# Sliding-window matmul on one core: other row blocks for the weight loads, and the last two k tiles split into two column halves

## Chip, core and metric

The kernel runs on one core of one Trainium2 chip. The metric is device time in microseconds of that core. The kernel before took 182.32 us in the median of three runs (182.32 to 182.44).

## The reference

```python
B, S, D, W = 4, 4096, 4096, 64          # x: [B, S, D] fp32, w: [D, D] fp32
for b in range(B):
    o = int(offsets[b])
    results.append(x[b, o:o+W] @ w)     # 64 rows of each batch times one 4096 x 4096 matrix
return np.stack(results)
```

There are only 256 rows of x, so every element of w is used 256 times and then dropped. The kernel must read 67.1 MB of w and 4.2 MB of x, and write 4.2 MB.

## The kernel before

Two groups g of 128 rows (two batches each) are transposed on PE. The weights stream from HBM, cast to fp16 by the load. k tiles 0 to 21 come in whole rows, in blocks of up to four k tiles; their products are added to an fp32 accumulator in SBUF on DVE. For the last ten k tiles ("tail") the columns are split into two groups of 2048, and each of the eight PSUM banks collects a whole tail.

```python
blocks = [(0, 1), (1, 1), (2, 4), (6, 4), (10, 4), (14, 4), (18, 2), (20, 2)]
k_tail = 22
wc_pool = ctx.enter_context(tc.tile_pool(name="wc", bufs=3))     # 4 k tiles each
w1_pool = ctx.enter_context(tc.tile_pool(name="w1", bufs=2))     # 1 k tile each
# ...
order = [1, 0]                       # column group 1 first, group 0 last
for ng in order:
    # ... loads on the GpSimd queue, two k tiles each; the last two of group 0 one by one
for ng in order:
    # ... matmuls: for ki, for g, for j (four banks for each g)
    for g in range(G):
        for j in range(n_sub):
            add_out(4 * g + j, g, ng * n_sub + j)            # acc += bank, on DVE
    for g in range(G):
        (nc.gpsimd if ng == order[0] else q[g]).dma_start(   # q = [nc.scalar, nc.sync]
            out=out[2 * g : 2 * g + 2, :, ng * NG : (ng + 1) * NG],
            in_=acc[g][:, ng * NG : (ng + 1) * NG],
        )
```

The stores of group 1 are issued on GpSimd, in the queue that holds the remaining loads. The stores of group 0 are the very last work, on ACT and SP.

## Time and profile before

| | before |
|---|---|
| time | 182.32 us |
| span in the profile | 180.4 us |
| PE / DVE / ACT busy | 127.1 / 79.2 / 14.4 us |
| share of the GpSimd DMA queue | 94.2% of 16 engines |
| HBM read / written | 71.30 / 4.19 MB |

Busy time of an engine says how much it did, not whether it was waited for. PE is busy for 70% of the span but waits for loads again and again. Time to landing runs from issue to the last engine's completion, so it includes queueing. And a stretch gives a mean of 16 engines, while a landing shows the latest of them.

### The profile page before, as it was taken

What the parts mean: (1) busy time and instruction counts of PE and PEld (TensorE: products, weight loads), DVE (VectorE), ACT (ScalarE), POOL (GpSimd) and SP (SyncE); (2) the same over time, 40 slices, a digit from 0 to 9 for tenths busy, and PEclk for the clock granted to TensorE, in tenths of its full rate; (3) what the DMA queues carried; (4) which work ended last, traced back from release to release, by engine and by line L of the source; (5) the groups of instructions that cost most, each with busy time, mean ns of one, the idle gap of its engine ahead of it and who ended that gap; (6) DMA issues with size and microseconds to landing.
All of it is one profiled execution on the core that took longest, in us unless ns stands there. A gap on an engine that the chain in (4) does not pass through costs nothing.

```text
span 180.4 us, 1501 instructions
## 1 busy us (share of the span) xinstructions
PE 127.1 (70%) x576; PEld 57.8 (32%) x576; DVE 79.2 (44%) x120; ACT 14.4 (8%) x19; POOL 15.2 (8%) x30
## 2 busy tenths in 40 slices
PE   0000789504999399908996599999789998898900
PEld 0000774101344144303442244444234443343400
DVE  0000667400587277811886167899920007300280
ACT  2422546400000000000000000000000000000000
POOL 4600000000000100020002400041011001100000
PEclk9999999965799999996999879999999999999975
DMA  5999989999998899999999999999999999999986
GB/s 185 314 254 216 273 189 196 236 233 225 233 233 174 182 233 233 238 218 233 196 196 203 225 207 207 225 193 214 215 213 216 213 214 214 216 212 214 362 367 265
DMA packets 4936, 40.98 MB, mean 227 GB/s; under 512 B 450, under 2 KB 450, under 8 KB 3010
## 3 DMA queue, kind: packets, MB, share of 16 engines
q0 software_dynamic: 4352, 36.70, 94.2%
q1 hardware_dynamic: 288, 2.10, 3.1%
q10 hardware_dynamic: 290, 2.10, 2.8%
q8 instruction: 4, 0.07, 0.1%
q14 instruction: 2, 0.02, 0.0%
HBM read 71.30 MB, written 4.19 MB: 419 GB/s over the span
## 4 chain that ended last, share of the span: by engine, by line
DMA 57%; PE 29%; another core or an unknown queue 5%; issue 3%; DVE 1%; POOLq 1%; POOL 1%; DVEq 1%
DMA wc<-in_w_dram 57%; PE bank L143 29%; DVE acc L153 1%; POOLq L68 1%; DVEq L227 1%; POOL xrow L75 0%; POOL identity masks.py:197 0%; POOLq L75 0%; DVEq L153 0%; POOL w L64 0%; POOLq masks.py:199 0%; POOLq L216 0%
## 5 line engine op out<-in xcount | busy, mean ns | idle before, releaser
L143 PE MATMUL bank<-wc,xT 128*128 128x512 f16 x448 | 106.0, 394 | 25.1 <-DMA wc<-in_w_dram 22.4
L153 DVE TENSOR_TENSOR acc<-acc,bank 128x512 f32<-128x512 f32 x104 | 68.1, 685 | 72.8 <-PE bank L143 72.2
L143 PEld LDWEIGHTS <-xT 128*128 128x128 f16 x512 | 51.2, 101 | 93.6 <-DMA wc<-in_w_dram 23.6
L129 PE MATMUL bank<-identity,xrow 128*128 128x128 f16 x64 | 7.1, 312 | 19.6 <-DMA xrow<-in_x_dram 19.6
L138 DVE CAST xT<-bank 128x512 f16<-128x512 f32 x8 | 5.5, 692 | 21.5 <-PE bank L129 21.5
L143 PE MATMUL bank<-w,xT 128*128 128x512 f16 x64 | 14.6, 385 | 0.0
L129 PEld LDWEIGHTS <-xrow 128*128 128x128 f16 x64 | 6.7, 148 | 19.8 <-issue 19.8
L108 POOL DMA_DIRECT2D wc<-in_w_dram x8 | 5.6, 710 | 42.4 <-PE bank L143 36.0
L92 POOL DMA_DIRECT2D wc<-in_w_dram x6 | 3.2, 545 | 67.7 <-PE bank L143 67.7
L168 DVE COPY acc<-bank 128x512 f32<-128x512 f32 x8 | 5.5, 692 | 1.6 <-PE bank L143 1.4
L140 ACT CAST xT<-bank 128x512 f16<-128x512 f32 x8 | 4.7, 585 | 8.2 <-PE bank L129 8.2
L170 ACT COPY acc<-bank 128x512 f32<-128x512 f32 x8 | 4.7, 585 | 2.5 <-PE bank L143 2.5
L198 POOL DMA_DIRECT2D out_dram<-acc x2 | 1.1, 536 | 18.5 <-DVE acc L153 18.5
L108 POOL DMA_DIRECT2D w<-in_w_dram x3 | 1.8, 607 | 8.6 <-DMA wc<-in_w_dram 8.6
L61 ACT CAST w<-acc 128x2048 f16<-128x2048 f32 x1 | 1.9, 1897 | 4.7 <-DMA acc<-in_w_dram 4.7
L75 POOL DMA_DIRECT2D xrow<-in_x_dram x4 | 2.1, 524 | 2.1 <-issue 2.1
L60 ACT CAST w<-acc 128x2048 f16<-128x2048 f32 x1 | 1.9, 1897 | 2.9 <-DMA acc<-in_w_dram 2.9
L60 ACT ACT_TABLE_LOAD x1 | 1.3, 1283 | 1.8 <-PEq L216 1.8
L64 POOL DMA_DIRECT2D w<-in_w_dram x1 | 0.7, 667 | 0.8 <-POOLq L216 0.8
masks.py:199 POOL TENSOR_SCALAR_AFFINE_SELECT identity<-identity 128x128 f16<-128x128 f16 x1 | 0.3, 287 | 0.1
masks.py:197 POOL MEMSET identity<- 128x128 f16 x1 | 0.2, 223 | 0.0
L216 POOL MEMSET const-float32-0.0<- 128x1 f32 x1 | 0.1, 99 | 0.4 <-issue 0.4
(3 smaller groups left out, 0.3 us busy)
## 6 DMA issues: line engine op xcount, KB each, us to landing
wc<-in_w_dram POOLq DMA_DIRECT2D x4, 4096.0 KB, 48.3
wc<-in_w_dram POOLq DMA_DIRECT2D x8, 1024.0 KB, 36.5
wc<-in_w_dram POOLq DMA_DIRECT2D x2, 2048.0 KB, 38.8
w<-in_w_dram POOLq DMA_DIRECT2D x2, 1024.0 KB, 28.2
xrow<-in_x_dram POOLq DMA_DIRECT2D x4, 512.0 KB, 14.5
out_dram<-acc POOLq DMA_DIRECT2D x2, 1024.0 KB, 19.3
acc<-in_w_dram SPq DMA_DIRECT2D x1, 1024.0 KB, 5.1
acc<-in_w_dram ACTq DMA_DIRECT2D x1, 1024.0 KB, 11.2
```

Of the source, the lines that this page charges most:

```text
L60: nc.scalar.copy(out=w_one[0][:, :NG], in_=w0_32[:, :NG])
L61: nc.scalar.copy(out=w_one[0][:, NG:], in_=w0_32[:, NG:])
L75: nc.gpsimd.dma_start(out=x16[g][m * WIN : (m + 1) * WIN, :], in_=x[b][bass.ds(o, WIN), :],)
L92: nc.gpsimd.dma_start(out=t[:, base : base + r * N], in_=w[k0 * P : (k0 + r) * P, :].rearrange("(p r) n -> p (r n)", r=r),)
L108: nc.gpsimd.dma_start(out=t[:, c : c + n * NG].rearrange("p (t n) -> p t n", t=n), in_=w[ki * P : (ki + n) * P, ng * NG : (ng + 1) * NG].r ...
L129: nc.tensor.matmul(out=ps[t][:, i * P : (i + 1) * P], lhsT=x_cols(g, 4 * t + i), rhs=identity[:], start=True, stop=True,)
L138: nc.vector.tensor_copy(out=dst, in_=ps[t][:])
L140: nc.scalar.copy(out=dst, in_=ps[t][:])
L143: nc.tensor.matmul(out=ps[bank][:], lhsT=xT[g][:, kt * P : (kt + 1) * P], rhs=rhs, start=start, stop=stop,)
L153: nc.vector.tensor_add(out=dst, in0=dst, in1=ps[bank][:])
L168: nc.vector.tensor_copy(out=acc[g][:, c * NT : (c + 1) * NT], in_=ps[bank][:])
L170: nc.scalar.copy(out=acc[g][:, c * NT : (c + 1) * NT], in_=ps[bank][:])
```

## The change

The intent has two parts: fewer, larger loads in whole rows with a shorter tail on fewer buffers, and a shorter end. At the end the last two k tiles are loaded, multiplied, added and stored in two column halves, so that the first half is stored while the second is still being worked on.

```diff
-    blocks = [(0, 1), (1, 1), (2, 4), (6, 4), (10, 4), (14, 4), (18, 2), (20, 2)]
-    k_tail = 22
+    blocks = [(0, 1), (1, 1), (2, 4), (6, 4), (10, 4), (14, 4), (18, 3), (21, 3)]
+    k_tail = 24
+    n_fine = 2
 ...
+    fine_steps.append((n_k - n_fine, n_fine, 0, NG // 2))
+    fine_steps += [(ki, 1, NG // 2, NG) for ki in range(n_k - n_fine, n_k)]
 ...                                      # group 1 is drained by DVE and ACT together:
+            add_out(4 * g + j, g, ng * n_sub + j)
+            nc.scalar.copy(out=tmp[2 * g + j // 2][:], in_=ps[4 * g + j + 1][:])
 ...                                      # group 0, k tiles 30 and 31:
+    for h in range(2):
+        js = range(h * n_sub // 2, (h + 1) * n_sub // 2)
+        for ki in range(k_fine, n_k):
             for g in range(G):
+                for j in js:
+                    tail_mm(ki, g, ng, j, False, ki == n_k - 1)
+        for g in range(G):
+            for j in js:
                 add_out(4 * g + j, g, ng * n_sub + j)
+            c0 = ng * NG + h * NG // 2
+            store(q[g], g, c0, c0 + NG // 2)
```

More of the change, by code (lines that the diff above doesn't have):

```diff
@@ L41 @@
     wc_pool = ctx.enter_context(tc.tile_pool(name="wc", bufs=3))
-    w1_pool = ctx.enter_context(tc.tile_pool(name="w1", bufs=2))
+    w1_pool = ctx.enter_context(tc.tile_pool(name="w1", bufs=1))
     acc_pool = ctx.enter_context(tc.tile_pool(name="acc", bufs=1))
@@ L49 @@
     xT = [x_pool.tile([P, D], fp16, name=f"xT{g}") for g in range(G)]
-    w_one = [w1_pool.tile([P, N], fp16, name="w1", tag="w1") for i in range(2)]
+    w_one = [w1_pool.tile([P, N], fp16, name=f"w1_{i}") for i in range(2)]
+    tmp = [acc_pool.tile([P, NT], fp32, name=f"tmp{i}") for i in range(4)]
     acc = [acc_pool.tile([P, N], fp32, name=f"acc{g}") for g in range(G)]
@@ L84 @@
     }
-    free = 0
     for k0, r in blocks[2:]:
-        if free < r:
-            t = wc_pool.tile([P, R_MAX * N], fp16, name="wc", tag="wc")
-            free = R_MAX
-        base = (R_MAX - free) * N
-        free -= r
+        t = wc_pool.tile([P, R_MAX * N], fp16, name="wc", tag="wc")
         nc.gpsimd.dma_start(
-            out=t[:, base : base + r * N],
+            out=t[:, : r * N],
             in_=w[k0 * P : (k0 + r) * P, :].rearrange("(p r) n -> p (r n)", r=r),
@@ L96 @@
         for q in range(r):
-            src[k0 + q] = lambda a, e, t=t, c=base + q * N: t[:, c + a : c + e]
+            src[k0 + q] = lambda a, e, t=t, c=q * N: t[:, c + a : c + e]
     tail = {}
     order = [1, 0]
-    for ng in order:
-        big = wc_pool.tile([P, R_MAX * N], fp16, name="wc", tag="wc")
-        small = w1_pool.tile([P, N], fp16, name="w1", tag="w1")
-        ki = k_tail
-        while ki < n_k:
-            n = 1 if ng == order[-1] and ki >= n_k - 2 else 2
-            n_in = (ki - k_tail) * NG
-            t, c = (big, n_in) if n_in < R_MAX * N else (small, n_in - R_MAX * N)
+    steps = [(ki, 2, 0, NG) for ki in range(k_tail, n_k, 2)]
+    fine_steps = steps[: -(n_fine // 2)]
+    fine_steps.append((n_k - n_fine, n_fine, 0, NG // 2))
+    fine_steps += [(ki, 1, NG // 2, NG) for ki in range(n_k - n_fine, n_k)]
+    for ng, st in zip(order, (steps, fine_steps)):
+        t = wc_pool.tile([P, R_MAX * N], fp16, name="wc", tag="wc")
+        pos = 0
+        for ki, n, c0, c1 in st:
+            wd = c1 - c0
             nc.gpsimd.dma_start(
-                out=t[:, c : c + n * NG].rearrange("p (t n) -> p t n", t=n),
-                in_=w[ki * P : (ki + n) * P, ng * NG : (ng + 1) * NG].rearrange(
+                out=t[:, pos : pos + n * wd].rearrange("p (t n) -> p t n", t=n),
+                in_=w[ki * P : (ki + n) * P, ng * NG + c0 : ng * NG + c1].rearrange(
                     "(t p) n -> p t n", p=P
@@ L114 @@
             for q in range(n):
-                tail[(ng, ki + q)] = t[:, c + q * NG : c + (q + 1) * NG]
-            ki += n
+                for j in range(wd // NT):
+                    a = pos + q * wd + j * NT
+                    tail[(ki + q, (ng * NG + c0) // NT + j)] = t[:, a : a + NT]
+            pos += n * wd
     def x_cols(g, kt):
@@ L177, with tail_mm @@
     whole_rows(last_block, range(order[1] * n_sub, (order[1] + 1) * n_sub), False)
-    q = [nc.scalar, nc.sync]
-    for ng in order:
-        kts = list(range(k_tail, n_k))
-        if ng == order[0]:
-            kts = list(last_block) + kts
-        for ki in kts:
-            for g in range(G):
-                for j in range(n_sub):
-                    c = ng * n_sub + j
-                    rhs = (
-                        src[ki](c * NT, (c + 1) * NT)
-                        if ki < k_tail
-                        else tail[(ng, ki)][:, j * NT : (j + 1) * NT]
-                    )
-                    mm(4 * g + j, g, ki, rhs, ki == kts[0], ki == kts[-1])
+    def tail_mm(ki, g, ng, j, start, stop):
+        c = ng * n_sub + j
+        rhs = src[ki](c * NT, (c + 1) * NT) if ki < k_tail else tail[(ki, c)]
+        mm(4 * g + j, g, ki, rhs, start, stop)
@@ L194, with store @@
+    out_rows = out.rearrange("b m n -> (b m) n")
+    def store(eng, g, c0, c1, cuts=(0, P)):
+        for a, e in zip(cuts, cuts[1:]):
+            eng.dma_start(out=out_rows[g * P + a : g * P + e, c0:c1], in_=acc[g][a:e, c0:c1])
+    ng = order[0]
+    kts = list(last_block) + list(range(k_tail, n_k))
+    for ki in kts:
         for g in range(G):
             for j in range(n_sub):
-                add_out(4 * g + j, g, ng * n_sub + j)
-        for g in range(G):
-            (nc.gpsimd if ng == order[0] else q[g]).dma_start(
-                out=out[2 * g : 2 * g + 2, :, ng * NG : (ng + 1) * NG],
-                in_=acc[g][:, ng * NG : (ng + 1) * NG],
-            )
+                tail_mm(ki, g, ng, j, ki == kts[0], ki == kts[-1])
@@ new lines @@
+    for g in range(G):
+        for j in range(0, n_sub, 2):
+            add_out(4 * g + j, g, ng * n_sub + j)
+            nc.scalar.copy(out=tmp[2 * g + j // 2][:], in_=ps[4 * g + j + 1][:])
+    for g in range(G):
+        for j in range(1, n_sub, 2):
+            c = ng * n_sub + j
+            dst = acc[g][:, c * NT : (c + 1) * NT]
+            nc.vector.tensor_add(out=dst, in0=dst, in1=tmp[2 * g + j // 2][:])
+        store(nc.gpsimd, g, ng * NG, (ng + 1) * NG)
+    ng = order[1]
+    k_fine = n_k - n_fine
@@ new lines @@
+    for ki in range(k_tail, k_fine):
+        for g in range(G):
+            for j in range(n_sub):
+                tail_mm(ki, g, ng, j, ki == k_tail, False)
+    q = [nc.scalar, nc.sync]
+    for h in range(2):
+        js = range(h * n_sub // 2, (h + 1) * n_sub // 2)
+        for ki in range(k_fine, n_k):
+            for g in range(G):
+                for j in js:
+                    tail_mm(ki, g, ng, j, False, ki == n_k - 1)
+        for g in range(G):
+            for j in js:
+                add_out(4 * g + j, g, ng * n_sub + j)
+            c0 = ng * NG + h * NG // 2
+            store(q[g], g, c0, c0 + NG // 2)
```

## The prediction

> **What bounds the kernel now.** I read the page's slices and DMA queues first, to see which resource has no slack; then the stretches of the last 16 us, then the landing times of the last transfers, and the chain of waits last of all, because a chain shows only one of several paths that end together.
>
> ```profile
> PE   0000789504999399908996599999789998898900
> DVE  0000667400587277811886167899920007300280
> DMA  5999989999998899999999999999999999999986
> HBM read 71.30 MB, written 4.19 MB: 419 GB/s over the span
> ```
>
> The DMA row never falls below 8 between the first slice and the last, while PE and DVE both have empty slices. So the 16 DMA engines carry the kernel from end to end. Loads that cast from fp32 to fp16 count in the GB/s row by what they write, half of what they read. Of the stretches (columns: window, its length, busy us and instructions of PE, PEld, DVE, ACT, POOL, then PE clock, DMA share, GB/s):
>
> ```profile
> 132.00:152.00 20.00, 19.81 (x92) 8.90 (x92) 2.05 (x5) 0.00 (x0) 0.54 (x1) 1.00 1.06 215
> 169.00:172.00 3.00, 2.79 (x13) 1.08 (x11) 1.69 (x3) 0.00 (x0) 0.00 (x0) 1.00 1.01 426
> 172.00:172.50 0.50, 0.00 (x0) 0.00 (x0) 0.50 (x2) 0.00 (x0) 0.00 (x0) 1.00 0.93 393
> 172.50:173.00 0.50, 0.00 (x0) 0.00 (x0) 0.50 (x2) 0.00 (x0) 0.00 (x0) 1.00 0.82 344
> 173.00:173.50 0.50, 0.00 (x0) 0.00 (x0) 0.50 (x2) 0.00 (x0) 0.00 (x0) 1.00 0.31 131
> 173.50:174.00 0.50, 0.00 (x0) 0.00 (x0) 0.50 (x2) 0.00 (x0) 0.00 (x0) 0.98 0.74 311
> 174.00:178.50 4.50, 0.00 (x0) 0.00 (x0) 1.19 (x2) 0.00 (x0) 0.00 (x0) 0.50 1.04 431
> ```
>
> In the middle the engines read 2 x 215 = 430 GB/s, and in the tail of pure stores they move 426 to 431 GB/s: one and the same rate. At it, 71.30 MB of loads and 4.19 MB of stores need 75.49 MB / 430 GB/s = 175.6 us of the span of 180.4 us. Only one hole shows, from 172.0 to 174.0 us: 393 + 344 + 131 + 311 = 1179 where four half microseconds at 431 would give 1724, so 545 / 431 x 0.5 = 0.63 us of the engines' mean time is lost there.
>
> The last transfers, by issue (timeline) and by time to landing (the DMA view of the stretch around each issue; the number at the end is us to landing):
>
> ```profile
> 135.63 0.54 POOL L108 DMA_DIRECT2D w<-in_w_dram  x1 [4.33 <-DMA wc<-in_w_dram]
> w<-in_w_dram POOLq DMA_DIRECT2D x1, 512.0 KB, 34.0
> 152.83 0.54 POOL L198 DMA_DIRECT2D out_dram<-acc  x1 [16.66 <-DVE acc L153]
> 155.22 0.53 POOL L198 DMA_DIRECT2D out_dram<-acc  x1 [1.85 <-DVE acc L153]
> out_dram<-acc POOLq DMA_DIRECT2D x1, 1024.0 KB, 19.3
> 172.83 0.35 ACTq L198 DMA_DIRECT2D out_dram<-acc  x1
> 175.21 0.35 SPq L198 DMA_DIRECT2D out_dram<-acc  x1
> out_dram<-acc ACTq DMA_DIRECT2D x1, 1024.0 KB, 4.2
> out_dram<-acc SPq DMA_DIRECT2D x1, 1024.0 KB, 4.2
> ```
>
> The last load (k tile 31) lands at 135.63 + 34.0 = 169.6 us. The two stores of the first column group, queued behind all loads, land at 172.1 and 174.5; the ACT store lands at 177.0 and the SP store at 179.4. These are steps of 2.4 to 2.5 us, and 1.049 MB at 430 GB/s is 2.44 us. So whichever engine finishes each transfer last had work all the way: the hole of 0.63 us was felt by engines that were ahead, not plainly by the one that sets the landings. From 179.4 to the end of the span is 1.0 us, and 1.9 us more lie between span and the measured 182.32 us.
>
> **What the Trainium skill says.** "DMA: Bandwidth & Descriptors", section "Where 436 GB/s comes from", puts the ceiling of the fabric at 435 GB/s; the trace's 426 to 431 agrees and says that no shuffling of transfers makes the middle faster. Its section "Issuing engines are not separate DMA queues" says that transfers from SP, ACT and GpSimd share the same 16 engines; the trace agrees, the two ACT and SP stores alone fill 174.0 to 178.5 us at 431 GB/s. Its section "Queues, rings and completion order" says that an engine goes round between the queues it has work for, packet by packet: stores issued earlier on ACT and SP will mix with those waiting in the GpSimd queue and push them later rather than end sooner in sum. In "Anatomy of one DMA" (SWDGE path) it gives about 2.0 us fixed plus bytes at 436 GB/s; that makes 4.4 us for 1.049 MB, and the trace has 4.2 us for the ACT and SP stores.
>
> **The change part by part.** (1) *Row blocks 4, 3, 3 in place of 4, 2, 2, tail of 8 k tiles in place of 10.* The bytes stay. Whole-row loads write 216 GB/s in the stretch from 81 to 98 us, the tail's form 215 from 132 to 152 us; moving 2 of 32 k tiles (4.19 MB, 9.75 us) between forms that differ by 0.5% is worth 0.05 us. (2) *Buffers.* The three big buffers now serve blocks 14-17, 18-20, 21-23, then the tail of group 1 waits for PE to finish 14-17 (117.3 us in the timeline) and that of group 0 for 18-20. Block 18-20 lands at 101.3 (the first matmul of block 14-17) + 20 x 3/4 = about 116; its 48 matmuls at 0.226 us (3.62 us for 16 in the timeline) start near 117.3 and end near 128.5. By then the queue holds work to 130.5 (21-23) and to 150 (four loads of 2.10 MB for group 1, 4.87 us each). So the group 0 loads are issued some 20 us before their turn: no starvation. (3) *Draining group 1 through ACT.* Four ACT copies (585 ns each in the page's groups) go beside four DVE adds, then four SBUF adds follow; PE loses less time at the group change, where it waited 12 times 0.22 us. But the next operands land at about 155 us and PE waits for them anyway. The GpSimd stores go out near 157 and 158.5 us instead of 152.8 and 155.2; their turn in the queue comes near 168 us. Worth 0. (4) *The tail in halves.* The three loads of k tiles 30 and 31 end when the two did, near 169.6 us. k tiles 28 and 29 land at 164.6 us; from there PE has the same 32 matmuls x 0.226 us = 7.2 us, ending near 171.9. The first add now follows the 21st of these instead of the 25th, near 169.5 instead of 170.31 us. Eight adds took 4.87 us, so 0.61 each: four end near 171.9, the other four near 174.4. The four half-size stores are issued near 170.8, 172.0, 173.2 and 174.4, in place of two at 172.83 and 175.21. The first enters while the GpSimd stores still drain, so the hole of 0.63 us is filled. Before, the ACT store's bytes began 0.7 us after issue (172.83 against the stretch from 173.5); so the last half has its bytes ready near 175.2. The half microseconds from 167.5 on show 270, 328 and 401 GB/s; with 213 for loads alone and 431 for stores alone, 0.74, 0.47 and 0.14 of them were loads, so the engines turn to stores at 167.5 + 0.5 x 1.35 = 168.2 us on average; by 175.2 they have moved 7.0 us x 430 = 3.0 MB, and 3.67 MB were on offer without the last half. The DMA engines are therefore never short, with 1.5 us to spare, and **the end is set by bytes**: between 0 (the slowest engine had no hole) and 0.63 us (all engines gain equally) earlier. (5) *Costs.* One more load, two more stores, and runs of 4 KB in place of 8 KB for the last two k tiles and the last stores, 4.2 MB together. From 64 KB runs (blocks of 4) to 8 KB runs (tail) the rate fell by the 0.5% of part 1; I put down 1% for this halving, 0.1 us of 9.75. Sum: 0.3 to 0.4 us gained of the hole (my middle between 0 and 0.63), 0.1 lost, nothing elsewhere: about 0.3 us.
>
> **Rivals.** *The tail is a latency chain.* The chain of waits speaks for it:
>
> ```profile
> 164.72 6.22 PE bank L143 x28
> 172.79 2.39 DVE acc L153 x4
> ```
>
> It runs from the last but one load through PE and DVE to the SP store, as if DMA were idle. Then the last issue comes 0.8 us sooner and a store of half the size takes 1.2 us less (2.0 + 1.2 = 3.2 us by the skill's fit, an estimate), and the end is 174.4 + 3.2 = 177.6 in place of 179.4: 1.8 us gained, 180.5 us. The landings at the full rate speak against it. *The queue runs dry in the middle*, because blocks of 3 come free later or a GpSimd issue waits for one of its older transfers. That would cost one step of up to 5 us, some 185 us; the 20 us of depth speak against it. *Smaller packets cost more than I put down.* Loads of 4 KB runs and stores of 4 KB rows carry 4.2 MB; at 5% less rate that is 0.5 us, giving 182.6.
>
> **Range and chances.** The middle is 182.32 - 0.3 = 182.0 us. The hole wholly filled and a little of the latency chain gives 181.3; smaller packets and no gain give 182.7. Faster by 2% would need 3.6 us, twice what the latency rival gives and more than all idle DMA time after 169 us: 2%. Slower by 2% needs a dry queue: 2%. Within 2%: 96%.
>
> **What would show it.** If I am right, the stretches from 172 to 174 us hold 400 GB/s or more, the SP and ACT stores are issued near 171, 172, 173 and 174.5 us, yet take far longer than 3.2 us from issue to landing, because they queue; the last load lands at 169.6 us within 0.3, and the last store between 178.7 and 179.5. I am wrong if the last store lands before 178.3, if a load's landing slips by more than 0.5 us, or if any middle slice of the DMA row falls under 8.

## The result

The changed kernel takes 182.38 us in the median of six runs (182.20 to 182.56), the kernel before 182.32 us (182.16 to 182.44). The ratio is 1.0004, with a 95% interval of 0.9991 to 1.0016. All ratios here are from runs of the same rounds, so they are not quite the ratios of the medians quoted. Medians of different rounds also come from different chips: the kernel before took 182.24 to 182.36 us on those used below. The kernel is correct, and the time is the same.

First the slices and the HBM line of the changed kernel.

```profile
PE   0000779504999399808995699999399999987900
DVE  0000657500578278802876168899374000820460
...
DMA  5999989999999899999989989999999999999994
...
HBM read 71.30 MB, written 4.19 MB: 418 GB/s over the span
```

The DMA row is full as before and the bytes are the same. Now the stretches at the end (columns: window, length, PE, PEld, DVE, ACT and POOL busy, PE clock, DMA share, GB/s), those of the changed kernel first:

```profile
172.00:172.50 0.50, 0.00 (x0) 0.00 (x0) 0.50 (x2) 0.00 (x0) 0.00 (x0) 1.00 0.85 360
172.50:173.00 0.50, 0.00 (x0) 0.00 (x0) 0.50 (x2) 0.00 (x0) 0.00 (x0) 1.00 1.02 426
173.00:173.50 0.50, 0.00 (x0) 0.00 (x0) 0.50 (x2) 0.00 (x0) 0.00 (x0) 1.00 1.01 418
173.50:174.00 0.50, 0.00 (x0) 0.00 (x0) 0.50 (x2) 0.00 (x0) 0.00 (x0) 1.00 0.99 410
...
177.50:178.00 0.50, 0.00 (x0) 0.00 (x0) 0.00 (x0) 0.00 (x0) 0.00 (x0) 0.50 0.85 344
178.00:178.50 0.50, 0.00 (x0) 0.00 (x0) 0.00 (x0) 0.00 (x0) 0.00 (x0) 0.50 0.40 164
178.50:179.00 0.50, 0.00 (x0) 0.00 (x0) 0.00 (x0) 0.00 (x0) 0.00 (x0) 0.50 0.16 66
179.00:179.50 0.50, 0.00 (x0) 0.00 (x0) 0.00 (x0) 0.00 (x0) 0.00 (x0) 0.50 0.04 16
```

And the kernel before in the same last stretches:

```profile
177.50:178.00 0.50, 0.00 (x0) 0.00 (x0) 0.00 (x0) 0.00 (x0) 0.00 (x0) 0.50 1.03 426
178.00:178.50 0.50, 0.00 (x0) 0.00 (x0) 0.00 (x0) 0.00 (x0) 0.00 (x0) 0.50 1.14 475
178.50:179.00 0.50, 0.00 (x0) 0.00 (x0) 0.00 (x0) 0.00 (x0) 0.00 (x0) 0.50 0.21 82
```

The hole of before, with its deepest half microsecond at 131 GB/s, is gone. But a ramp has appeared at the end: 344, 164, 66 and 16 GB/s over the last 2 us, where the kernel before ran at full rate up to 178.5 us. The idle time was moved, not removed.

The trace shows for which engine. It keeps 16 completion counts for each full transfer, one from each engine: a store of 120 rows that is tried below has 15 after its issue, and one of 8 rows has 8. No view prints these counts; they were read from the packed trace, one execution of each kernel. Their first and last, in us:

| | last load | GpSimd stores (group 1) | ACT and SP stores (group 0) |
|---|---|---|---|
| before | 168.05 to 169.63 | 170.55 to 172.12, 173.01 to 174.56 | 176.54 to 177.01, 179.05 to 179.46 |
| changed | 168.21 to 169.81 | 170.72 to 172.27, 173.17 to 174.71 | 174.43 to 175.96, 175.66 to 177.21, 176.93 to 178.47, 178.16 to 179.70 |

The engines run some 1.5 us apart. In the kernel before, the latest count goes from 174.56 to 177.01 us, 2.45 us, like the steps for 1.05 MB around it (2.44 to 2.49): the latest engine had no hole. The earliest count takes 3.53 us for that step: the hole was in the engines that were ahead. In the changed kernel the engines that are ahead no longer wait there, and the 1.5 us stay to the end. The mean of the 16 counts of the last store comes 0.5 us sooner (178.62 in place of 179.16 us), the latest does not (179.70 and 179.46).

Next the issues of the last transfers in the changed kernel (timeline) and, in the second fence, their times to landing (DMA view of the stretch around each).

```profile
140.37 0.54 POOL L108 DMA_DIRECT2D wc<-in_w_dram  x1 [4.50 <-DMA wc<-in_w_dram]
158.35 0.54 POOL L189 DMA_DIRECT2D out_dram<-acc  x1 [17.45 <-DVE acc L205]
159.56 0.53 POOL L189 DMA_DIRECT2D out_dram<-acc  x1 [0.67 <-DVE acc L205]
170.89 2.74 ACTq L189 DMA_DIRECT2D out_dram<-acc  x2
172.08 2.72 SPq L189 DMA_DIRECT2D out_dram<-acc  x2
```

```profile
wc<-in_w_dram POOLq DMA_DIRECT2D x1, 256.0 KB, 29.4
out_dram<-acc POOLq DMA_DIRECT2D x1, 1024.0 KB, 13.9
out_dram<-acc POOLq DMA_DIRECT2D x1, 1024.0 KB, 15.2
out_dram<-acc ACTq DMA_DIRECT2D x1, 512.0 KB, 5.1
out_dram<-acc SPq DMA_DIRECT2D x1, 512.0 KB, 5.2
```

The last load lands at 140.37 + 29.4 = 169.8 us. The GpSimd stores land at 172.3 and 174.8. A row of two issues, such as 172.08 with 2.72 us, covers both, so the second SP issue starts near 172.08 + 2.72 - 0.35 = 174.45 us (0.35 us is one issue in the trace before), and its store lands at 174.45 + 5.2 = 179.65 us. It took 4.2 us before for twice the bytes. The smaller store is slower from issue to landing because it waits in line.

The chain of waits of the changed kernel, in order of time, still ends with PE and DVE, like the one before:

```profile
164.84 5.36 PE bank L144 x24
170.20 1.35 DVE acc L154 x3
...
172.65 1.79 DVE acc L154 x3
```

It ends at 174.4 us, 0.7 us sooner than the one before (175.2 us), and what it releases is a store of half the size; yet the end did not move. This view alone would have promised a gain.

### The profile page after: what moved, and what is told of

It reads as the page before. It is cut to its first block, busy times and chain, and to the rows that moved or that the text cites. A ratio compares the mean times of both kernels' runs of the same rounds, so it can differ in the third digit from the quotient of the medians.

```text
span 180.6 us, 1505 instructions
## 1 busy us (share of the span) xinstructions
PE 125.7 (70%) x576; PEld 58.1 (32%) x576; DVE 80.5 (45%) x120; ACT 16.5 (9%) x23; POOL 14.5 (8%) x29
## 4 chain that ended last, share of the span: by engine, by line
DMA 63%; PE 26%; issue 3%; DVE 2%; POOL 1%; POOLq 1%; DVEq 0%
DMA wc<-in_w_dram 63%; PE bank L144 26%; DVE acc L154 2%; POOL wc L108 1%; POOLq L70 1%; POOL xrow L77 0%; DVEq L251 0%; POOL identity masks.py:197 0%; POOLq L77 0%; POOL w L66 0%; POOLq masks.py:199 0%; DVEq L154 0%; POOLq L240 0%
## 5 line engine op out<-in xcount | busy, mean ns | idle before, releaser
L144 PE MATMUL bank<-wc,xT 128*128 128x512 f16 x480 | 111.6, 396 | 26.2 <-DMA wc<-in_w_dram 26.2
L154 DVE TENSOR_TENSOR acc<-acc,bank 128x512 f32<-128x512 f32 x100 | 67.0, 686 | 70.7 <-PE bank L144 70.0
L200 ACT COPY tmp<-bank 128x512 f32<-128x512 f32 x4 | 2.1, 600 | 119.9 <-PE bank L144 119.9
L89 POOL DMA_DIRECT2D wc<-in_w_dram x6 | 3.2, 542 | 88.2 <-PE bank L144 88.2
L108 POOL DMA_DIRECT2D wc<-in_w_dram x10 | 6.7, 683 | 36.0 <-PE bank L144 26.4
L144 PE MATMUL bank<-w,xT 128*128 128x512 f16 x32 | 7.2, 382 | 0.0
L205 DVE TENSOR_TENSOR acc<-acc,tmp 128x512 f32<-128x512 f32 x4 | 2.5, 681 | 0.0
L66 POOL DMA_DIRECT2D w<-in_w_dram x1 | 0.7, 660 | 0.8 <-POOLq L240 0.8
```

Source lines behind the costliest of these rows:

```text
L89: nc.gpsimd.dma_start(out=t[:, : r * N], in_=w[k0 * P : (k0 + r) * P, :].rearrange("(p r) n -> p (r n)", r=r),)
L108: nc.gpsimd.dma_start(out=t[:, pos : pos + n * wd].rearrange("p (t n) -> p t n", t=n), in_=w[ki * P : (ki + n) * P, ng * NG + c0 : ng * NG ...
L144: nc.tensor.matmul(out=ps[bank][:], lhsT=xT[g][:, kt * P : (kt + 1) * P], rhs=rhs, start=start, stop=stop,)
L154: nc.vector.tensor_add(out=dst, in0=dst, in1=ps[bank][:])
L205: nc.vector.tensor_add(out=dst, in0=dst, in1=tmp[2 * g + j // 2][:])
```

## The experiments

The theory: the time is the bytes at the rate of the DMA engines, and the engine that ends last has no hole to fill. The main rival: the tail is a chain of load, PE, adds and store, and the change shortens it. A second rival: the halves gain and the new blocks lose the same.

### One part at a time

`halves_only` keeps the old blocks, buffers and drain of group 1, and splits only the last two k tiles:

```diff
 # kernel before
+            st = st[:-1] + [(n_k - 2, 2, 0, NG // 2)]
+            st += [(ki, 1, NG // 2, NG) for ki in range(n_k - 2, n_k)]
 # and the loop over h of the changed kernel for matmuls, adds and stores of group 0
```

> Only the split of the last two k tiles into column halves, on the old row blocks and buffers. Bytes theory (the DMA engine that runs latest has work without a hole from the first load to the last store, so the time is bytes at 430 GB/s): 182.2 to 182.5 us, as both kernels; the hole from 172 to 174 us is filled, and the last store still lands between 179.3 and 179.8 us. Latency-chain theory (the tail is load, PE, adds, store): 180.5 us. Cancelling theory (the halves gain and the new blocks lose the same): 180.5 to 181.7 us here, and over 182.9 us for the run with the blocks alone.

`blocks_only` has the new blocks, buffers and drain of group 1, and the old end:

```diff
 # changed kernel
-    fine_steps.append((n_k - n_fine, n_fine, 0, NG // 2))
-    fine_steps += [(ki, 1, NG // 2, NG) for ki in range(n_k - n_fine, n_k)]
+    fine_steps += [(ki, 1, 0, NG) for ki in range(n_k - n_fine, n_k)]
 # and two whole stores of group 0 after all eight adds
```

> Only the new row blocks, the tail of 8 k tiles, the buffers and the drain of group 1 through ACT; the last group ends as in the kernel before, with two whole stores. Bytes theory: 182.2 to 182.5 us, with the hole near 173 us back in the stretches and the last store landing near 179.4 us. Cancelling theory: 182.9 us or more.

Measured: 182.40 us (ratio 1.0001, 0.9987 to 1.0014) and 182.31 us (0.9997, 0.9983 to 1.0011). Neither part gains or loses more than the 0.25 us that these intervals resolve. The second rival falls: nothing is cancelled. The latency-chain rival falls for the full kernel too, as the halves alone should have given 180.5 us. The trace of `blocks_only` has the hole back:

```profile
172.50:173.00 0.50, 0.00 (x0) 0.00 (x0) 0.50 (x2) 0.00 (x0) 0.00 (x0) 1.00 0.62 262
173.00:173.50 0.50, 0.00 (x0) 0.00 (x0) 0.50 (x2) 0.00 (x0) 0.00 (x0) 1.00 0.27 115
```

So a hole of this depth comes and goes with the halves, without any effect on the time.

### Taking the backlog away

If the halves do shorten the chain, and only the backlog of bytes hides it, then the gain must appear once the backlog is gone. Both kernels were run without the GpSimd stores of group 1. Half of the output is then missing.

```diff
 # kernel before
-            (nc.gpsimd if ng == order[0] else q[g]).dma_start(
+            if ng == order[1]:
+                q[g].dma_start(
 # changed kernel
-        store(nc.gpsimd, g, ng * NG, (ng + 1) * NG)
```

> The kernel before without the two GpSimd stores of group 1 (2.10 MB; half of the output is missing on purpose). Those bytes are 4.9 us at 430 GB/s. With them gone the DMA engines have no backlog at the end, and the latency chain alone sets it: the SP store is still issued at 175.2 us, 0.9 us to its first bytes, 2.44 us for 1.05 MB and 0.4 to 0.8 us of spread between engines, landing near 179.1: 182.0 us (181.6 to 182.3). A kernel bound by bytes alone without any chain would give 177.5 us. In other words I expect this kernel's chain and its bytes to end within 0.5 us of each other.

> The changed kernel without the two GpSimd stores of group 1 (wrong on purpose, as its partner). Now the halves can show what they save on the chain: last issue at 174.4 us, 0.9 us to first bytes, 1.2 us for 0.52 MB, 0.4 to 0.8 us of spread: landing at 177.0 to 177.4, 179.7 to 180.1 us, some 2.0 us less than the partner. If the halves were worth nothing for any other reason (a slower chain, costlier packets), the two would again be equal.

Measured: 182.18 us (182.07 to 182.29, ratio 0.9986) and 180.09 us (179.95 to 180.24, ratio 0.9872). The old end gained 0.2 us from 2.10 MB less, the new end 2.3 us. Stretches of the old end without the stores:

```profile
168.00:173.50 5.50, 4.03 (x19) 1.65 (x17) 2.94 (x5) 0.00 (x0) 0.00 (x0) 1.00 0.07 13
173.50:179.00 5.50, 0.00 (x0) 0.00 (x0) 1.93 (x4) 0.00 (x0) 0.00 (x0) 0.65 0.92 381
```

and of the new end without them:

```profile
168.00:171.50 3.50, 3.50 (x18) 1.46 (x15) 2.11 (x4) 0.00 (x0) 0.00 (x0) 1.00 0.10 19
171.50:176.50 5.00, 0.22 (x2) 0.00 (x0) 2.76 (x5) 0.00 (x0) 0.00 (x0) 0.96 1.00 403
```

Without the stores the DMA engines stand almost idle for 5.5 us in one and 3.5 us in the other while PE and DVE finish. The new end is worth 182.18 - 180.09 = 2.1 us here, the gain it was made for. In the real kernels the stores of group 1 fill that idle time, 4.9 us of bytes, and leave nothing to gain. The old kernel's chain and its bytes end within 0.2 us of each other.

The new end without the backlog also shows where the ramp comes from:

```profile
176.00:176.50 0.50, 0.00 (x0) 0.00 (x0) 0.00 (x0) 0.00 (x0) 0.00 (x0) 0.57 0.99 401
176.50:177.00 0.50, 0.00 (x0) 0.00 (x0) 0.00 (x0) 0.00 (x0) 0.00 (x0) 0.50 0.44 164
177.00:177.50 0.50, 0.00 (x0) 0.00 (x0) 0.00 (x0) 0.00 (x0) 0.00 (x0) 0.50 0.00 0
```

The same last store ends here without a ramp: its 16 counts lie within 0.15 us (177.08 to 177.22), though those of the last load still lay 1.7 us apart (167.90 to 169.60). So the spread is not made by these stores. It is carried in from the loads, and it was gone after all engines had stood idle.

### Adding bytes far from the end

```diff
 # changed kernel, ahead of the first matmul with weights
+    nc.sync.dma_start(out=x16[0].bitcast(fp32)[:], in_=w[(n_k - 1) * P : n_k * P, :NG])
```

> The changed kernel with one more load of 1.05 MB that nobody reads, on the SP queue, into rows of x that PE has already transposed (issued near 26 us, 145 us before the tail). Bytes theory: a transfer anywhere costs its own time at 430 GB/s, 2.44 us: 184.8 us (184.5 to 185.1). If the DMA row's 8s and the waits of PE in the middle are slack in which a transfer hides: 182.4 us.

Measured: 184.86 us (184.68 to 185.00), 2.48 us over the 182.38 us of the changed kernel, which was not run beside it, and 2.62 us over the kernel before in the same rounds (182.24 us); expected were 2.44. The load was issued at 22.18 us:

```profile
22.18 0.33 SPq L143 DMA_DIRECT2D xrow<-in_w_dram  x1
...
174.27 2.73 SPq L191 DMA_DIRECT2D out_dram<-acc  x2
```

Nobody waits for it, and PE waits for loads around it anyway; yet it moved the last stores from 172.08 to 174.27 us. So bytes put near the start cost their full time too.

### The same bytes in another order

```diff
 # changed kernel
-        store(nc.gpsimd, g, ng * NG, (ng + 1) * NG)
+        store([nc.scalar, nc.sync][g], g, ng * NG, (ng + 1) * NG)
```

> The changed kernel with the two stores of group 1 on ACT and SP in place of GpSimd; same bytes. They are issued near 158 us, when all loads are already queued on GpSimd. If the DMA engines take turns between queues packet by packet, the stores overtake the remaining loads, the last load lands up to 4.9 us later (174.5), and the chain after it, without backlog, takes what it took in the run without these stores: 180.09 + 4.88 = 185.0 us (184.0 to 185.3). If transfers are served in order of arrival, the stores still come after the loads: 182.4 us. The bytes alone, without the chain, would say 182.4 us in either case.

Measured: 187.85 us (187.61 to 188.32), ratio 1.0313. The direction was right and the size was not: 2.8 us more than expected. The stores did overtake. They landed 12.3 and 11.7 us after issue, and the last load slipped to 140.59 + 34.6 = 175.2 us, against 140.24 + 29.4 = 169.6 us in the run without these stores. That is 5.6 us, 0.7 more than their bytes. The remainder is on PE. Its groups in `early_stores` (timeline) are

```profile
159.93 3.61 PE L144 MATMUL bank<-wc,xT 128*128 128x512 f16 x16 [1.34 <-DMA wc<-in_w_dram]
170.30 8.63 PE L144 MATMUL bank<-wc,xT 128*128 128x512 f16 x32 [6.75 <-DMA wc<-in_w_dram]
```

and in the run without the stores

```profile
159.78 3.61 PE L144 MATMUL bank<-wc,xT 128*128 128x512 f16 x16 [1.29 <-DMA wc<-in_w_dram]
164.66 7.07 PE L144 MATMUL bank<-wc,xT 128*128 128x512 f16 x32 [1.27 <-DMA wc<-in_w_dram]
```

PE waited 6.75 us in one piece, and the stretch from 168 to 173 us has a granted clock of 0.50; the 32 last matmuls took 8.63 in place of 7.07 us. The Trainium skill, "TensorE: Matmul & The Clock Gate", section "Part 1: The HAM clock gate", says that the clock falls to half after an idle window of about 3.4 us. The trace agrees roughly: the clock fell 3.1 us after the last matmul (163.55 to 166.68 us) and rose 3.2 us after the next (170.30 to 173.51 us); in the changed kernel a pause of 3.0 us was already enough (127.17 to 130.18 us, half clock from 129.47 us). Together 5.6 + 1.6 = 7.2 us of the 187.85 - 180.09 = 7.8 us are accounted for; the last 0.5 us fell after the last landing (184.4 us in a span of 185.8 us, against 177.2 in 178.1), and what caused it was not tried. So the same bytes in this order cost 187.85 - 182.38 = 5.5 us more than in the order of the changed kernel. The bytes are a floor, and the changed kernel is at it only because transfers that nobody waits for come after those that somebody waits for.

### The engine that ends last

In the changed kernel the 16 engines end up to 1.5 us apart. If the latest could be spared some work, that might be a gain. Rows 0 to 119 of the last store spread over 15 engines: of its 16 counts one came at the issue (174.6 us) and 15 from 177.9 us on.

```diff
 # changed kernel
-            store(q[g], g, c0, c0 + NG // 2)
+            store(q[g], g, c0, c0 + NG // 2, (0, 120, P) if h == 1 and g == 1 else (0, P))
```

> The changed kernel with the very last store cut into rows 0 to 119 and rows 120 to 127, so that the first piece spreads over 15 DMA engines of 8 rows each and leaves one engine without work of it. In the changed kernel the engines end up to 1.5 us apart. If the engine left out is the one that ends last, the last landing comes 0.1 to 0.4 us sooner, 182.1 us; if it is another, nothing or 0.15 us later, 182.4 to 182.6 us. The effect is near what five rounds resolve, so the stretches after 177.5 us decide as well.

Measured: 182.89 us (182.51 to 182.98), ratio 1.0035. This missed the range by 0.3 us, so it was run again beside the unaltered changed kernel and a cut at row 64, `(0, 64, P)`, which makes the same number of transfers but spreads them evenly.

> The changed kernel unaltered, as the base for the two cuts on the same chip, since the run with the cut at row 120 came out at 182.89 us, 0.3 us over the range I had given it. 182.2 to 182.5 us.

> The cut at row 120 once more. If the 0.3 us were chance of that chip, 182.3 to 182.6 us and within 0.1% of the unaltered kernel; if they are the cut's, 182.7 to 183.0 us again.

> The last store cut at row 64: one transfer more, as with the cut at 120, but both pieces spread over all 16 engines. If the uneven spread costs the time, this is as the unaltered kernel, 182.2 to 182.5 us; if the further transfer costs it (one more issue of 1 us on SP, one more completion), 182.7 to 183.0 us like the cut at 120.

Measured: 182.32 us unaltered (ratio 1.0002), 182.83 us with the cut at 120 (1.0031, 1.0017 to 1.0044), 182.45 us with the cut at 64 (1.0004). So the loss belongs to the uneven spread, not to the further transfer. The last stretch of the repeated cut at 120 shows one more late piece:

```profile
178.50:179.00 0.50, 0.00 (x0) 0.00 (x0) 0.00 (x0) 0.00 (x0) 0.00 (x0) 0.50 0.27 107
179.00:179.50 0.50, 0.00 (x0) 0.00 (x0) 0.00 (x0) 0.00 (x0) 0.00 (x0) 0.50 0.08 33
179.50:180.20 0.70, 0.00 (x0) 0.00 (x0) 0.00 (x0) 0.00 (x0) 0.00 (x0) 0.50 0.02 6
```

6 GB/s for 0.7 us is 4.2 KB, one row of 1024 fp32 values. The counts agree: the piece of 120 rows ended at 179.96 us and that of eight at 180.16. The eight rows thus went to engines that include a late one. The latest count came 1.26 us after that of the transfer before, as in the changed kernel (1.23 to 1.26), so it is that of an engine with a full share, and the engine that was spared was not the latest. This profile is of the slowest of the five executions (183.11 us); that of the first run is of its fastest (182.51 us), and its pieces end at 179.50 and 179.55 us. One row is only 4.1 KB / (430 / 16 GB/s) = 0.15 us of an engine at the mean rate, so the size of the loss, 0.5 us, is not explained. Which engines are late, and why they fell behind, stays open. A version that beats both kernels was not found.

## Why the prediction was right

The time, 182.38 us, lies in the range of 181.3 to 182.7 us, 0.4 us above the middle of 182.0. The mechanism was right, that the end is set by bytes; the gain of 0.3 us that was forecast did not come, and the range held only because it also allowed for no gain.

- *The bound.* Bytes at 430 GB/s: confirmed by the further load (2.5 to 2.6 us for 2.44 predicted) and by both parts alone (182.40 and 182.31 us). The prediction calls its rate in agreement with a ceiling that lies on the side of SBUF; only the stores show that (426 to 431 GB/s), as the loads of the middle read 430 GB/s but write 215 into SBUF.
- *Part 1 and 2, blocks and buffers, worth 0.05 us and no starvation.* Right: `blocks_only` is equal. The GpSimd issues for group 0 began at 127.5 us, where I had put 128.5, and no middle slice of the DMA row fell under 8.
- *Part 3, the drain through ACT, worth 0.* Right: the stores of group 1 were issued at 158.35 and 159.56 us, a microsecond later than I worked out, and still landed where the queue put them.
- *Part 4, the tail.* The issues at 170.89, 172.08, about 173.3 and 174.45 us are within 0.1 us of those worked out. The last load landed at 169.8 us, within the 0.3 us allowed. The mean of the four half microseconds from 172 us is 403 GB/s, so the hole was filled, though the first of them, at 360, is under the 400 named. But the last store landed at 179.65 us, outside the 178.7 to 179.5 I had named. Of the two ends I gave for the gain, 0 and 0.63 us, I took the middle; the counts show that 0 was right, for the reason given there: the engine that sets the landing had no hole (2.45 us from 174.56 to 177.01 us in the kernel before). The filled hole came back as the ramp after 177.5 us. The term mis-sized is thus "0.3 to 0.4 us gained of the hole"; it measured nothing.
- *Part 5, costs of 0.1 us.* Not resolved; the intervals are 0.13% wide on either side, or 0.24 us.
- *The latency rival.* It named a real gain: 1.8 us estimated, 2.1 us measured, but only where the backlog is taken away.
- *The dry-queue rival.* Refuted by the full DMA row. *The smaller packets* at 5% less rate would have made 182.6 us, the upper end of the measured interval; a smaller cost cannot be told from none.

## What to carry to other kernels

When a chain of waits and a backlog of transfers end at the same time, shortening one of them gains nothing; work out both, and take one away in a throwaway run to see what the other is worth. Before speeding up a tail, add up the bytes that must still be moved after the last load and compare them with the time the chain needs. A hole in the mean of 16 engines is a gain only if the latest engine shares it; and transfers that nobody waits for belong behind those that somebody does.

## What the Trainium skill lacked or had wrong

- "DMA: Bandwidth & Descriptors", section "Anatomy of one DMA": the fit of 2.0 us plus bytes at 436 GB/s is for the GpSimd path, and there is none for ACT and SP. Their stores without the GpSimd backlog landed in 2.8 to 2.9 us for 0.52 MB and 3.9 to 4.0 us for 1.05 MB, 0.4 us less than the fit's 3.2 and 4.4.
- The same page gives no figure for how far apart the 16 engines end one evenly spread transfer. Here it depends on what came before: 0.15 us after the engines had stood idle, 1.54 us behind a backlog, and that made a hole of 0.63 us worthless. In "Latency and other measured facts" it calls engines 7 and 15 usually slower. The traces here do not number the engines, so no run tests that; but in the kernel before the spread stayed between 1.5 and 1.6 us from 101 to 174.6 us, so in that time the latest engine did not keep losing ground to the earliest.
- The same page, "Queues, rings and completion order": the turns between queues agree with the run in which stores overtook loads (11.7 to 12.3 us to landing). It gives no cost for mixing; there the loads slipped 5.6 us for 4.9 us of stores.
- No page gives the rate of the first load: in the kernel before it was 180, 229 and 328 GB/s in the half microseconds from 2.0, 2.5 and 3.0 us, and 410 GB/s only from 4.0 us.
